# A seven-product w_up: another order of the products, w_down groups between the units, x1 kept in DRAM

## The chip, the cores and the metric

The kernel runs on one core of one Trainium2 chip. Its engines are TensorE (PE in the profile; PEld is its weight load), VectorE (DVE), ScalarE (ACT), GpSimd (POOL) and SyncE (SP, which issues most loads). The metric is the device time of one execution in microseconds.

## The reference

One layer of a hybrid backbone is computed for 128 context tokens and 512 latent tokens, 640 rows of 1024 channels: adaLN-modulated norm, retention and grouped-query attention side by side, a merge, an output projection w_out with a gated residual; then a second modulated norm and a gated MLP with a width-3 convolution between up- and down-projection; a final norm. The change lies in the second half:

```python
xs = xs + g1 * y                                        # y = merged mixers @ w_out
h = rmsnorm(xs, norm2_g[l]) * (1.0 + sc2) + sh2         # h2 in the kernel
xs = xs + g2 * conv_ffn(h, w_up[l], conv_w[l], conv_b[l], w_down[l])
y_sample = rmsnorm(xs, final_g)

def conv_ffn(h, w_up, conv_w, conv_b, w_down):          # D_FF = 2816
    u = h @ w_up                                        # 1024 x 5632: halves a and g
    up = jnp.pad(u, ((0, 0), (1, 1), (0, 0)))
    uc = conv_w[0] * up[:, :L] + conv_w[1] * up[:, 1:L + 1] + conv_w[2] * up[:, 2:L + 2] + conv_b
    a, g = jnp.split(uc, 2, axis=-1)
    return (jax.nn.silu(g) * a) @ w_down
```

## The kernel before, in words

Every float32 product is made of three matmuls on a high and a low part of each operand (high x high, high x low, low x high). A weight block arrives by SyncE as a `raw` tile of 1 MB (two of them). The high part is a ScalarE cast (L146); the low part `raw - hi` is either a VectorE subtraction (L151) or, in the mode "dma", a scaled ScalarE copy (L148) and an accumulating DMA from GpSimd's queue (L149). High and low parts lie in `wh` tiles of [128, 1024], of which there are eight.

*w_out, second half, and h2.* For each of five token tiles (t = 0 is the context) a PSUM bank collects eight k steps, four from each half of the weights (`out_half(t, h)`). `evac_out` multiplies by the gate and adds to x1, the residual; `h2_norm` scales the row; `h2_trans` transposes it on TensorE (L1047), and ScalarE and VectorE write the modulated high and low parts (L1055 to L1059) into `h2`, from which w_up reads. Meanwhile the w_up blocks of the first pair of feature tiles (`whl`, `w_g`) are loaded and split, and the pair's products (`up_cols`, L1118 to L1120) are mixed with the last transposes.

*w_up.* The 22 feature tiles of each half (i = 0 for a, i = 1 for g) are worked in eleven pairs p. Pairs 0 and 1 are plain products. VectorE forms sums of blocks of h2 (`diff`, `neg_sum`, L1168 to L1174) and for p = 2 to 10 a pair and half is one *unit*: a product of 2x2 blocks done with seven products of half size instead of eight. Each product is 12 matmuls of 322 columns (L1307, L1309, L1310) on a weight operand that VectorE and ScalarE prepare (L1285, L1288, L1293; for products 2 and 3 ScalarE and GpSimd's DMA, L1290, L1291). Products 1, 6, 7 and 4 are added up in one bank without clearing it, and between any two ScalarE has to copy what stands there (L1312, L1316, L1320, L1324), so that each next product waits for a copy. Product 2 has a bank of its own, 5 and 3 share one. The order is 1, 5, 6, 2, 7, 3, 4.

*conv and gate.* When both i of a feature tile are there, `conv` (one ScalarE pass, two on VectorE) and `gate` follow: tanh, two VectorE multiplications (L1139, L1140), the high part by ScalarE (L1141) and the low part by GpSimd (L1142).

*w_down.* Four feature tiles (two for p = 0 and 1 alone) are a group of rows; for each of two column halves five banks of 128 x 512 are summed over them, and `down_add` multiplies each bank by the gate and adds it to x1. All groups but the last stand in a list with the w_up groups: `plain(1,0)`, the two halves of the first w_down group, `plain(1,1)`, then unit(p,0), for odd p both halves of a w_down group, unit(p,1). A final w_down group and the closing norm (L1236 and following) come after the list.

*Order.* TensorE runs this list as written (`manual_schedule`). After each item `pump` loads the next block and prepares weights ahead as long as eight `wh` slots allow, and one waiting conv or gate is taken from the queue `later`. The order on the other engines is a scheduler's.

## Time and profile before

| | us |
|---|---|
| median of 3 runs | 1221.78 (1220.73 to 1225.39) |
| profiled execution | 1221.7, its span on the core 1219.9 |
| mean granted TensorE clock | 0.990 |
| busy: PE, DVE, ACT, POOL | 1165.2, 773.4, 553.9, 201.5 |
| w_out second half, h2, first pair of w_up | 709 to 772.5 |
| gate rows on TensorE | 772.5 to 776 |
| plain(1,0) | 776 to 794.6 |
| first w_down group | 794.6 to 808.6 |
| plain(1,1) | 808.6 to 822.9 |
| 18 units and four w_down groups of ten banks | 822.9 to 1176.5 |
| last w_down | 1176.5 to 1204.6 |
| closing norm and outputs | 1204.6 to 1219.9 |

Times within the span count from its start. A tile has its pool's name, its own and a number (mm7.mm.40 is the 40th bank of the pool mm7). Engines with a q (POOLq) are their queues of DMAs.

### The profile page before, as it was taken

How to read it: one execution, taken by the hardware profiler on the slowest of the kernel's cores; microseconds unless marked ns; L12 is line 12 of the kernel's file. 1: busy time of each engine (PE TensorE's matmuls, PEld its weight loads, DVE VectorE, ACT ScalarE, POOL GpSimd, SP SyncE). 2: the span in 40 equal slices, each digit the busy share in tenths (PEclk: the TensorE clock that was granted, in tenths of full speed). 3: DMA queues.
4: the chain of work that ended last, by engine and by line, in shares of the span. 5: the costliest groups of instructions: out<-in, count | busy, mean ns of one | idle time of the engine just before them, and what ended most of it. 6: DMA issues, size and time to landing. Idle time of an engine off the chain costs nothing.

```text
span 1219.9 us, 18328 instructions
## 1 busy us (share of the span) xinstructions
PE 1165.2 (96%) x7329; PEld 1046.6 (86%) x7329; DVE 773.4 (63%) x1450; ACT 553.9 (45%) x999; POOL 201.5 (17%) x184
## 2 busy tenths in 40 slices
PE   4999999999999999999999997999999999999994
PEld 3788899999988888789999887999898898898984
DVE  5676977763344346544233368889788787797877
ACT  4355655551223234434222334637457266474553
POOL 0032200000022000231111110203223122122222
PEclk9999999999999999999999998999999999999998
DMA  8822111126544422022222417235756568457522
GB/s 285 277 96 70 36 35 35 36 74 213 183 164 139 154 80 75 4 70 68 71 70 70 155 39 86 78 87 113 173 104 137 115 118 182 97 110 175 105 70 86
DMA packets 127413, 132.20 MB, mean 108 GB/s; under 512 B 25936, under 2 KB 96672, under 8 KB 127328
## 3 DMA queue, kind: packets, MB, share of 16 engines
q1 hardware_dynamic: 104432, 109.01, 28.3%
q0 software_dynamic: 22176, 20.71, 11.6%
q8 instruction: 57, 0.93, 0.3%
q10 hardware_dynamic: 720, 1.31, 0.3%
q14 instruction: 28, 0.23, 0.1%
HBM read 107.69 MB, written 3.41 MB: 91 GB/s over the span
## 4 chain that ended last, share of the span: by engine, by line
PE 74%; DVE 13%; ACT 4%; issue 4%; DMA 3%; POOL 1%; SPq 0%; DVEq 0%; ACTq 0%; POOLq 0%
DVE x1.u1.1_6381 L1218 1%; DMA weights.raw.199_7284<-in_w_up 1%; DMA weights.wh.244_8024<-weights.raw.232_7804 1%; DMA weights.raw.366_10197<-in_w_down 0%; DMA weights.raw.324_9445<-in_w_down 0%; DMA weights.raw.282_8693<-in_w_down 0%; DMA xin.u1.1_112<-in_x_sample 0%; DMA weights.raw.404_10963<-in_w_down 0%; POOL f0.s.5_3525 L901 0%; DVE weights.raw.216_7428 L1285 0%; DVE gt.gt0.5_7252 L1170 0%; DVE gt.gt0.5_7252 L1168 0%; DVE x1.u1.1_6381 L1236 0%; ACT const.u1.1_70 L1320 0%; PE mm1.mm.11_318 L158 0%
## 5 line engine op out<-in xcount | busy, mean ns | idle before, releaser
L790 POOL TENSOR_TENSOR ret.r2k.6_3635<-ret.u5.5_3528,ret.u1.1_3521 128x256 f32<-128x256 f32 x2 | 1.4, 740 | 205.1 <-ACT ret.u5.5_3528 L786 205.1
L1321 DVE TENSOR_TENSOR t7.u3.3_6921<-t7.u3.3_6921,const.u1.1_70 128x322 f32<-128x322 f32 x9 | 8.1, 895 | 10.0 <-ACT const.u1.1_70 L1320 10.0
L524 POOL TENSOR_TENSOR p1.u1.1_618<-p1.u3.3_622,p1q.u1.1_612 128x512 f32<-128x512 f32 x1 | 1.3, 1337 | 59.3 <-DMA p1.vc.6_627<-in_cache_v 59.3
L839 DVE SCALAR_TENSOR_TENSOR ret2.u1.1_4322<-ret2.u1.1_4322,const.u14.14_94 64x128 f32<-64x128 f32 x24 | 6.8, 338 | 6.6 <-ACT ret2.u1.1_4322 L832 6.5
L151 DVE TENSOR_TENSOR weights.wh.183_6567<-weights.raw.181_6564,weights.wh.182_6566 128x1024 fp32r<-128x1024 f32 x1 | 1.2, 1224 | 14.3 <-ACT weights.wh.182_6566 L146 14.3
L1233 POOL TENSOR_TENSOR x1.u1.1_6381<-x1.u1.1_6381,weights.raw.409_10973 128x512 f32<-128x512 f32 x5 | 7.5, 1493 | 15.2 <-ACT x1.tm.122_11171 L1223 7.1
L355 PE MATMUL mm1.mm.1_180<-const.u1.1_70,xin.u1.1_112 128*128 128x128 f32 x4 | 1.1, 435 | 9.1 <-DVE xin.u1.1_112 L348 9.1
L841 DVE SCALAR_TENSOR_TENSOR ret2.u1.1_4322<-ret2.u1.1_4322,const.u14.14_94 64x128 f32<-64x128 f32 x24 | 6.6, 382 | 4.8 <-ACT ret2.u1.1_4322 L834 4.8
L792 DVE TENSOR_TENSOR ret.u5.5_3528<-ret.u5.5_3528,ret.u1.1_3521 128x512 f32<-128x512 f32 x5 | 3.5, 693 | 9.4 <-POOL ret.r2k.8_3706 L790 3.3
L792 DVE TENSOR_TENSOR ret.u4.4_3527<-ret.u4.4_3527,ret.u1.1_3521 128x512 f32<-128x512 f32 x5 | 3.5, 692 | 9.0 <-POOL ret.r2k.11_3886 L790 4.7
L392 ACT CAST acts.u1.1_100<-f0.s.1_113 128x640 fp32r<-128x640 f32 x4 | 2.9, 728 | 12.8 <-DVE f0.s.1_113 L390 12.8
L355 PEld LDWEIGHTS mm1.mm.1_180<-const.u1.1_70,xin.u1.1_112 128*128 128x128 f32 x4 | 0.7, 217 | 9.3 <-DVE xin.u1.1_112 L348 9.3
L149 POOL DMA_DIRECT2D weights.wh.207_7299<-weights.raw.200_7286 x1 | 0.8, 849 | 45.1 <-ACT weights.wh.207_7299 L148 45.1
L828 POOL DMA_DIRECT2D out_new_state_ret_fwd<-ret.r2k.25_4345 x1 | 0.7, 654 | 43.8 <-ACT ret.r2k.25_4345 L827 43.8
L151 DVE TENSOR_TENSOR weights.wh.108_4352<-weights.raw.106_4349,weights.wh.107_4351 128x1024 fp32r<-128x1024 f32 x1 | 1.2, 1225 | 10.3 <-ACT weights.wh.107_4351 L146 10.3
L901 POOL TENSOR_TENSOR f0.s.5_3525<-f0.s.5_3525,ret2.ny20.11_4904 128x512 f32<-128x512 f32 x5 | 6.0, 1236 | 9.1 <-DVE ret2.ny20.11_4904 L218 9.1
L392 ACT CAST acts.u1.1_100<-f0.s.2_114 128x640 fp32r<-128x640 f32 x4 | 2.9, 730 | 9.8 <-DVE f0.s.2_114 L390 9.8
L258 DVE COPY mod2.wr.9_4312<-aux3.aux.15_4279 128x128 f32<-128x128 f32 x1 | 0.3, 291 | 10.9 <-PE aux3.aux.15_4279 L255 10.9
L493 ACT ACTIVATE f0.s.3_724<-f0.s.3_724,p1q.ny20.11_892 128x128 f32<-128x128 f32 x20 | 6.0, 388 | 2.5 <-DVE p1q.ny20.11_892 L216 2.5
L146 ACT CAST weights.wh.112_4507<-weights.raw.111_4505 128x1024 fp32r<-128x1024 f32 x1 | 1.1, 1050 | 13.3 <-PE mm3.mm.36_4220 L159 13.3
L924 POOL TENSOR_TENSOR f0.s.5_3525<-f0.s.5_3525,ret.r2k.56_4795 128x512 f32<-128x512 f32 x1 | 1.3, 1284 | 33.5 <-DVE ret.r2k.56_4795 L922 33.5
L974 DVE SCALAR_TENSOR_TENSOR rt.thr.6_5935<-rt.thr.6_5935,mm3.mm.71_6118 128x320 f32<-128x320 f32 x1 | 0.5, 489 | 9.6 <-PE mm3.mm.71_6118 L195 9.6
(7045 smaller groups left out, 4947.9 us busy)
## 6 DMA issues: line engine op xcount, KB each, us to landing
xin.u1.1_112<-in_x_sample SPq DMA_DIRECT2D x4, 512.0 KB
p0.u5.5_130<-in_w_mod SPq DMA_DIRECT2D x2, 1024.0 KB
p0.u6.6_135<-in_w_mod SPq DMA_DIRECT2D x2, 1024.0 KB
p0.u7.7_138<-in_w_mod SPq DMA_DIRECT2D x2, 1024.0 KB
mod.wm.2_2921<-in_w_mod SPq DMA_DIRECT2D x1, 2048.0 KB
mod.wm.4_3072<-in_w_mod SPq DMA_DIRECT2D x1, 2048.0 KB
mod.wm.6_3227<-in_w_mod SPq DMA_DIRECT2D x1, 2048.0 KB
mod.wm.8_3382<-in_w_mod SPq DMA_DIRECT2D x1, 2048.0 KB
```

The source lines that it names most:

```text
L151: (lo_eng or V).tensor_sub(lo, rv, hi.bitcast(F32))
L355: nc.tensor.transpose(ps[:, j * P:(j + 1) * P], xin[:, t, k * P:(k + 1) * P], ident)
L392: nc.scalar.copy(hT[0][:, k, :], xk)
L493: nc.scalar.activation(x[:, j], x[:, j], AF.Copy, scale=rstd[:, j:j + 1])
L790: nc.gpsimd.tensor_mul(sw[:, :, b * 32:(b + 1) * 32], xs, r1[:, t, 1:2, b * 32:(b + 1) * 32].to_broadcast([P, 8, 32]))
L792: V.tensor_mul(z, z, r1[:, t, 0:1, :].to_broadcast([P, 8, 64]))
L839: V.scalar_tensor_tensor(Ss[0:64, hh, st + 1, j], Ss[0:64, hh, st, j], cdsel[0:64, h:h + 1], Ss[0:64, hh, st + 1, j], op0=ALU.mult, op1=AL ...
L841: V.scalar_tensor_tensor(Ss[64:128, hh, 2 - st, j], Ss[64:128, hh, 3 - st, j], cdsel[64:128, h:h + 1], Ss[64:128, hh, 2 - st, j], op0=ALU. ...
L901: nc.gpsimd.tensor_mul(ov, ov, rso[:, 4 * t:4 * t + 4].unsqueeze(2).to_broadcast([P, 4, P]))
L1218: V.tensor_add(x1[:, t, gs], x1[:, t, gs], tm)
L1233: nc.gpsimd.tensor_mul(x1[:, t, lo], x1[:, t, lo], fg[:, lo])
L1321: V.tensor_sub(u[1][:, hi_u], u[1][:, hi_u], u3[i])
```

## The change

1. w_out's second half goes in plain order: after the first two half banks each tile's two halves follow one another. The part `whl` of the first w_up block is split into 1280 and 768 columns and made during the first two tiles, the latter in a new kind of x1 tile (`x_row`, four of 768 columns, which also hold the conv results); it takes no `wh` slots any more.
2. As soon as a tile of x1 is final after w_out it is also written to DRAM (`x1d`, from GpSimd's queue). The first w_down group overwrites x1 by a ScalarE copy (`step` 0), the next groups add to it (`step` 1), and the group at p = 9 adds, multiplies once by the gate and adds the part of `x1d` that GpSimd's queue reads back (`step` 2). The last group after the list keeps `down_add`. x_tmp has three buffers instead of four.
3. The low part of a gate is made on VectorE instead of GpSimd. The gates of odd pairs run after the second w_down half.
4. The low parts of the plain(1,0) and plain(1,1) weights are made in the mode "dma".
5. The two halves of a w_down group stand apart: plain(1,0), half, plain(1,1), half; unit(p,0), half, unit(p,1), half. Preparations are sorted by the first use.
6. The products go 1, 5, 6, 2, 3, 7, and product 4 is held until two items of the following group have run.

In the changed file lines move by up to 25: L1030 is L1036, L1036 is L1042, L1058 and L1059 are L1064 and L1065; of a unit's copies L1312, L1314, L1316, L1320 and L1324 are L1329, L1331, L1333, L1337 and L1342, its casts and DMAs L1288 to L1291 are L1305 to L1308; the conv's ScalarE pass L1128 is L1133.

VectorE where token tile 3 is normed (nm1, ni1, ny1, nt1 belong to its rsqrt; tm.43 is an x_tmp tile of token tile 4), before:

```order
L1036 TENSOR_TENSOR x1.u2.2_6382<-x1.u2.2_6382 128x1
L1030 TENSOR_TENSOR x1.tm.43_6859<-mm3.mm.88_6773,gate.u1.1_5311 128x512
L206 TENSOR_SCALAR x1.nm1.39_6832<-x1.u2.2_6382 128x1
L151 TENSOR_TENSOR weights.wh.202_7289<-weights.raw.199_7284,weights.wh.201_7288 128x1024
L207 TENSOR_SCALAR x1.ni1.40_6833<-x1.nm1.39_6832 128x1
L1031 TENSOR_TENSOR x1.u1.1_6381<-x1.u1.1_6381,x1.tm.43_6859 128x512
L208 TENSOR_SCALAR x1.ny1.41_6834<-x1.ni1.40_6833 128x1
L209 TENSOR_SCALAR x1.nm1.39_6832<-x1.nm1.39_6832 128x1
```

and after the change:

```order
L1042 TENSOR_TENSOR x1.u2.2_6382<-x1.u2.2_6382 128x1
L1064 CAST acts.u1.1_100<-x1.row.40_6818 128x4x128
L206 TENSOR_SCALAR x1.nm1.41_6826<-x1.u2.2_6382 128x1
L1065 TENSOR_TENSOR acts.u2.2_101<-x1.row.40_6818,acts.u1.1_100 128x4x128
L207 TENSOR_SCALAR x1.ni1.42_6827<-x1.nm1.41_6826 128x1
L208 TENSOR_SCALAR x1.ny1.43_6828<-x1.ni1.42_6827 128x1
L209 TENSOR_SCALAR x1.nm1.41_6826<-x1.nm1.41_6826 128x1
L212 SCALAR_TENSOR_TENSOR x1.nt1.44_6829<-x1.ny1.43_6828,x1.nm1.41_6826 128x1
```

The subtraction L151 on the weights of plain(1,0) no longer stands inside this norm.

ScalarE at the start of unit(6,1) (mm.40 is its shared bank, mm.41 that of product 5, mm.37 the shared bank of unit(6,0)), before:

```order
L1312 COPY t7.u2.2_6920<-mm7.mm.40_9335 128x322
L1314 ACTIVATE t7.u4.4_6922<-mm7.mm.41_9353 128x322
L1316 ACTIVATE t7.u4.4_6922<-mm7.mm.40_9335 128x322
L1288 CAST weights.wh.318_9350<-weights.raw.308_9161 128x512
L1288 CAST weights.wh.319_9368<-weights.raw.308_9161 128x512
```

and after the change:

```order
L1329 COPY t7.u2.2_6928<-mm7.mm.40_9263 128x322
L1305 CAST weights.wh.314_9278<-weights.raw.308_9162 128x512
L1331 ACTIVATE t7.u4.4_6930<-mm7.mm.41_9281 128x322
L1305 CAST weights.wh.315_9296<-weights.raw.298_8969 128x512
L1342 COPY t7.u1.1_6927<-mm7.mm.37_9144 128x322
L1305 CAST weights.wh.317_9316<-weights.raw.308_9162 128x512
L1133 ACTIVATE x1.row.82_9319<-t7.u1.1_6927,t7.u5.5_6935 128x641
L1333 ACTIVATE t7.u4.4_6930<-mm7.mm.40_9263 128x322
```

The copies after products 1 and 6 of a unit (L1329, L1333) now have product 5's and the previous unit's product 4's between them.

GpSimd around the w_down group of p = 7 (raw.316 and raw.324, in the changed kernel raw.316 and raw.327, are the two halves of the w_down weights), before:

```order
L149 DMA weights.wh.326_9523<-weights.raw.316_9308 128x1024
L1142 TENSOR_TENSOR gt.gt1.20_9440<-t7.cv.42_9310,gt.gt0.19_9439 128x641
L149 DMA weights.wh.328_9528<-weights.raw.316_9308 128x1024
L1142 TENSOR_TENSOR gt.gt1.20_9440<-t7.cv.43_9331,gt.gt0.19_9439 128x641
L149 DMA weights.wh.331_9596<-weights.raw.324_9445 128x1024
L149 DMA weights.wh.333_9601<-weights.raw.324_9445 128x1024
L1291 DMA weights.wh.338_9702<-weights.raw.329_9532 128x4x128
```

and after the change:

```order
L149 DMA weights.wh.322_9438<-weights.raw.316_9299 128x1024
L149 DMA weights.wh.324_9443<-weights.raw.316_9299 128x1024
L1308 DMA weights.wh.331_9586<-weights.raw.325_9447 128x4x128
L1308 DMA weights.wh.332_9636<-weights.raw.325_9447 128x4x128
L149 DMA weights.wh.335_9673<-weights.raw.327_9470 128x1024
L149 DMA weights.wh.337_9678<-weights.raw.327_9470 128x1024
```

The gates' low parts have left the queue, and the two halves' DMAs have those of the unit between them. The core of the diff:

```diff
+    dp = Pool("spill", space=bass.MemoryType.DRAM)
+    x1d = dp([P, NT, DM])
...
     def x_tmp():
-        return x1p([P, 512], tag="tm", bufs=4)
+        return x1p([P, 512], tag="tm", bufs=3)
+
+    def x_row(dtype=F32):
+        return x1p([P, 768], dtype, tag="row", bufs=4)
...
-    whl = [[x[:, :1024] for x in gt_flat(F32R)]]
-    nc.scalar.copy(whl[0][0], raw[:, :1024])
-    V.tensor_sub(whl[0][1], raw[:, :1024], whl[0][0].bitcast(F32))
+    whl = [[x[:, :1280] for x in gt_flat(F32R)], [x_row(F32R) for _ in range(2)]]
...
         for t in range(NT):
-            if t in (1, 2, 3):
-                out_half(t + 1, 0)
+            if t >= 2:
+                out_half(t, 0)
             out_half(t, 1)
             evac_out(1)(t, bank[t])
-            if t == 3:
-                whl.append([wp([P, 1024], F32R, tag="wh", bufs=8) for _ in range(2)])
-                nc.scalar.copy(whl[1][0], raw[:, 1024:])
-                V.tensor_sub(whl[1][1], raw[:, 1024:], whl[1][0].bitcast(F32))
+            nc.gpsimd.dma_start(x1d[:, t, :], x1[:, t, :])
+            if t in (0, 1):
+                rv = raw[:, 1280 * t:1280 + 768 * t]
+                nc.scalar.copy(whl[t][0], rv)
+                V.tensor_sub(whl[t][1], rv, whl[t][0].bitcast(F32))
...
-        nc.gpsimd.tensor_sub(r[1], ca, r[0].bitcast(F32))
+        V.tensor_sub(r[1], ca, r[0].bitcast(F32))
...
+    def down_sum(ps, t, c0, step):
+        gs = slice(c0, c0 + 512)
+        if step == 0:
+            nc.scalar.copy(x1[:, t, gs], ps)
+            return
+        V.tensor_add(x1[:, t, gs], x1[:, t, gs], ps)
+        if step == 2:
+            xr = x_tmp()
+            nc.gpsimd.dma_start(xr, x1d[:, t, gs])
+            V.tensor_mul(x1[:, t, gs], x1[:, t, gs], gb[:, t == 0, gs])
+            V.tensor_add(x1[:, t, gs], x1[:, t, gs], xr)
...
-            st["w"] = w_split(st["raw"], 8, 256)
+            st["w"] = w_split(st["raw"], 8, 256, "dma")
...
-        order = (1, 5, 6, 2, 7, 3, 4)
+        order = (1, 5, 6, 2, 3, 7, 4)
...
-    groups = [plain_group(1, 0)] + down_groups([0, 1]) + [plain_group(1, 1)]
+    d0 = down_groups([0, 1], 0)
+    groups = [plain_group(1, 0), d0[0], plain_group(1, 1), d0[1]]
     for p in range(2, NF // 2):
-        groups.append(unit_group(p, 0))
+        groups += [unit_group(p, 0), unit_group(p, 1)]
         if p % 2:
-            groups += down_groups(list(range(2 * p - 4, 2 * p)))
-        groups.append(unit_group(p, 1))
-    seq = [x for g in groups for x in g[2]]
+            d = down_groups(list(range(2 * p - 4, 2 * p)), 2 if p == 9 else 1, (2 * p + 1, 2 * p))
+            groups = groups[:-1] + [d[0], groups[-1], d[1]]
+    seq, held = [], []
+    for _, _, items in groups:
+        for x in items[:-1] if len(items) == 7 else items:
+            seq.append(x)
+            held = [(n - 1, y) for n, y in held]
+            if held and held[0][0] == 0:
+                seq.append(held.pop(0)[1])
+        if len(items) == 7:
+            held.append((2, items[-1]))
+    seq += [y for _, y in held]
...
+    preps.sort(key=lambda z: z[4])
```

More of the change, by code (lines that the diff above doesn't have):

```diff
@@ L1134, in gate @@
     def gate(f):
+        if f // 2 not in gts:
+            gts[f // 2] = gt_pair()
         r = [x[:, f % 2, :641] for x in gts[f // 2]]
@@ L1322, in go @@
                     V.memset(u[1][:, 642:643], 0)
+                    later.append(lambda: conv(f0_ + 1, i))
                 elif m == 4:
@@ L1326, in go @@
                     later.append(lambda: conv(f0_, i))
-                    if i:
-                        later.append(lambda: gate(f0_))
+                    if i and (p % 2 == 0):
+                        later.extend([lambda: gate(f0_ + 1), lambda: gate(f0_)])
                 else:
@@ L1358, in go @@
                     down_mm(ps, t, fs, st["w"])
-                    down_add(ps, t, g * 512)
+                    down_sum(ps, t, g * 512, step)
+                    if g and t == NT - 1:
+                        later.extend([lambda f=f: gate(f) for f in after])
                 return go
@@ L1384, in pump @@
             elif preps and preps[0][0] < loaded and sum(z for z, last in live if last >= n) + preps[0][2] <= 8:
-                gi, fn, tiles, last = preps.pop(0)
+                gi, fn, tiles, last, _ = preps.pop(0)
                 fn()
```

17 lines of the change are left out of this document (5 added, 12 removed).

## The prediction

> **What bounds the kernel now.** I read the page, then windows by stage, then what TensorE waits for.
>
> ```profile
> PE 1165.2 (96%) x7329; PEld 1046.6 (86%) x7329; DVE 773.4 (63%) x1450; ACT 553.9 (45%) x999; POOL 201.5 (17%) x184
> PE 74%; DVE 13%; ACT 4%; issue 4%; DMA 3%; POOL 1%; SPq 0%; DVEq 0%; ACTq 0%; POOLq 0%
> ```
>
> In the windows a row has the stretch, its length, the busy time of PE, PEld, DVE, ACT and POOL, the granted clock (PEclk, third from the end), the DMA share and GB/s:
>
> ```profile
> 740.00:760.00 20.00, 16.72 (x114) 16.72 (x115) 16.87 (x49) 6.25 (x17) 0.00 (x0) 0.83 0.73 48
> 776.00:794.60 18.60, 16.18 (x99) 15.92 (x98) 12.16 (x13) 10.55 (x15) 7.90 (x4) 0.91 0.56 141
> 822.90:1176.50 353.60, 341.85 (x1993) 314.17 (x1993) 285.64 (x449) 205.22 (x353) 88.98 (x69) 1.00 0.61 129
> 1176.50:1204.60 28.10, 28.10 (x134) 23.08 (x132) 22.48 (x41) 11.24 (x23) 9.61 (x6) 1.00 0.00 1
> ```
>
> PE is the bound, 96% busy, and both kernels give it the same number of instructions. Only its waits, and the granted clock behind them, can be won. The order of the engines' instructions is the same up to about 700 us. From there PE is short of its time in the h2 stage (740 to 760), in the first plain w_up product (776 to 794.6) and in the unit stage; the last w_down has no wait, and neither that nor the closing norm changes.
>
> ```profile
> PE aux3.aux.97_6973 L1047 <- DVE gt.gt1.2_6393 L1038: 4.8, 1, 4.8
> PE mm7.mm.5_7312 L1120 <- DVE weights.wh.204_7293 L151: 2.4, 1, 2.4
> PE aux3.aux.95_6864 L1047 <- DVE gt.gt0.1_6392 L1038: 1.4, 1, 1.4
> ...
> PE mm7.mm.55_10223 L1307 <- ACT const.u1.1_70 L1320: 1.1, 1, 1.1
> ...
> PE mm7.mm.40_9335 L1307 <- ACT t7.u2.2_6920 L1312: 1.1, 1, 1.1
> ```
>
> The first three waits belong to the two early stages. The other two kinds are the units': product 6 waits until ScalarE has copied product 1 out of the bank (L1312), product 4 until it has copied product 7 (L1320). What this costs is read from lengths:
>
> ```profile
> 863.30:891.50 28.20, 28.12 (x122) 22.50 (x121) 20.44 (x31) 7.21 (x12) 2.36 (x3) 1.00 0.55 123
> 945.30:973.20 27.90, 27.90 (x123) 22.60 (x122) 20.68 (x33) 7.38 (x12) 2.34 (x3) 1.00 0.54 125
> 973.20:985.60 12.40, 12.40 (x86) 12.40 (x85) 9.54 (x17) 8.16 (x16) 3.84 (x3) 1.00 0.64 128
> 985.60:998.80 13.20, 12.68 (x85) 12.42 (x85) 13.16 (x21) 9.79 (x18) 3.97 (x3) 1.00 0.47 107
> 998.80:1013.00 14.20, 12.90 (x86) 12.38 (x85) 12.20 (x23) 9.19 (x18) 4.08 (x4) 1.00 0.53 109
> 1013.00:1027.20 14.20, 13.13 (x87) 12.56 (x86) 9.99 (x14) 12.19 (x18) 6.20 (x6) 1.00 0.95 183
> 1027.20:1055.00 27.80, 27.80 (x121) 22.53 (x121) 20.67 (x33) 7.33 (x12) 2.30 (x3) 1.00 0.53 123
> 1109.10:1136.90 27.80, 27.80 (x121) 22.52 (x121) 20.66 (x33) 7.33 (x12) 2.31 (x3) 1.00 0.53 123
> ```
>
> The four w_down stretches take 28.2 + 27.9 + 27.8 + 27.8 = 111.7 us, the 18 units the rest of 353.6: 241.9. A unit right behind w_down takes 12.40 without a wait (seven products of 1.77, below), the others 13.2 to 14.2. Excess: 241.9 - 18 x 12.40 = 18.7 us. Listed waits alone show less, because each matmul row reaches over the start of the next.
>
> **The change, part by part.** *w_out and h2.* The weights of the first plain product (weights.raw.199) land at 737.14, VectorE's low-half subtraction L151 waits for the cast of them, and the norm of token tile 3 is queued behind it on VectorE:
>
> ```profile
> 729.84 7.30 DMA weights.raw.199_7284<-in_w_up
> 738.30 1.23 DVE L151 TENSOR_TENSOR weights.wh.202_7289<-weights.raw.199_7284,weights.wh.201_7288 128x1024 fp32r<-128x1024 f32 x1 [1.47 <-ACT weights.wh.201_7288 L146]
> 743.30:747.40 4.10, 4.10 (x20) 4.10 (x21) 4.03 (x17) 1.50 (x4) 0.00 (x0) 0.50 0.83 6
> 720.30:752.00 31.70, 25.49 (x154) 22.78 (x153) 26.53 (x85) 14.38 (x30) 2.00 (x6) 0.89 0.65 70
> 751.99 0.45 PE aux3.aux.99_7049 L1047 x4
> ```
>
> Behind the 4.8 us of waiting the clock is 0.50 for 4.1 us, which loses 2.05. In the new order that L151 is gone (the low half is a ScalarE pass and a GpSimd DMA that nothing on VectorE waits for), and tiles 2 and 3 end half a w_out bank earlier. ScalarE, 14.38 busy of 31.70, has room for the pass. Recoverable: 1.4 + 4.8 + 2.05 = 8.2 us. But VectorE is the next limit: of 31.70 us up to the last tile's transposes (751.99) it is busy 26.53, and 1.23 of that leaves: 720.3 + 25.3 = 745.6. PE's own work there is 25.49, 2.05 of it lost to the clock, so it would be ready at 743.7 and is not the limit; w_g's low halves (one landed 9.3 us after its issue, row below) may come a microsecond late, which these 1.9 us cover. Gain 751.99 - 745.6 = **6.4** (bounds: 3, if half moves to the next tile's norm, and 8.2). I take VectorE's value, as it leaves that engine no idle time.
>
> *First plain product.* The 2.4 us wait for L151 (which sits behind VectorE's operand sums) and the half clock behind it:
>
> ```profile
> 779.58 1.15 DVE weights.wh.204_7293 L151
> 781.70:785.10 3.40, 3.40 (x15) 3.40 (x14) 3.40 (x4) 1.24 (x3) 3.40 (x2) 0.50 0.92 240
> weights.wh.196_6936<-weights.raw.194_6933 POOLq DMA_DIRECT2D x1, 512.0 KB, 9.3
> ```
>
> 2.4 + 1.7 = **4.1**. The raw slot is free early now, all four low halves can be made during the h2 stage, and even a DMA of 9.3 us has 30. Bounds 0 and 4.1; I take the upper one, since nothing that it waits for is near.
>
> *Units.* Order 1 5 4' 6 2 3 7 (4' of the unit before) puts two products, 3.5 us, between any two of the shared bank instead of one. Behind a w_down group only product 5 stands between 1 and 6, as in the 12.40 unit of before, which shows no wait; 7 and 4 are then two w_down banks apart.
>
> ```profile
> 985.59 0.31 PE L1307 MATMUL mm7.mm.37_9190<-acts.u1.1_100,weights.wh.301_9048 128*128 128x322 f32 x1
> 987.37 0.30 PE L1307 MATMUL mm7.mm.38_9212<-sums.u1.1_6910,weights.wh.302_9066 128*128 128x322 f32 x1
> L148 ACT ACTIVATE weights.wh.326_9523<-weights.raw.316_9308 128x1024 fp32r<-128x1024 f32 x1 | 1.1, 1067 | 0.0
> L1312 ACT COPY t7.u2.2_6920<-mm7.mm.34_9051 128x322 f32<-128x322 f32 x1 | 0.4, 427 | 0.7 <-PE mm7.mm.34_9051 L1310 0.7
> ```
>
> A product takes 1.77 (985.59 to 987.37, less the odd 0.01). The copy takes 0.43 and may stand behind one or two weight passes of up to 1.07 on ScalarE: 2.6 at most, under 3.5. Only two links keep a stall: the last unit's 4 directly behind its 7 (0.8: copy, semaphore and restart), and four times the gate of the pair before a w_down group, whose low half I find 0.3 late (1.2). I leave 1.7 for what I cannot place: 18.7 - 0.8 - 1.2 - 1.7 = **15.0** (bounds 0 and 18.7).
>
> *VectorE's load.* In the unit stage w_down's 80 two-input operations become 60 (three groups with one add, p = 9 with three, ScalarE copies in the plain stage): -20 x 0.68. Sixteen gate low halves of 641 columns come to it from GpSimd, as long as a gate multiplication: +16 x 0.82. But GpSimd's were not free for it:
>
> ```profile
> 989.47 0.68 DVE L1285 TENSOR_TENSOR weights.raw.300_9046<-weights.raw.300_9046 128x512 f32<-128x512 f32 x1
> 990.08 0.82 DVE L1140 TENSOR_TENSOR t7.cv.36_8825<-t7.cv.36_8825,t7.cv.38_9163 128x641 f32<-128x641 f32 x1
> 992.25 2.66 DVE L1285 TENSOR_TENSOR weights.raw.300_9046<-weights.raw.300_9046 128x512 f32<-128x512 f32 x2
> 991.80 1.97 POOL L1142 TENSOR_TENSOR gt.gt1.18_9156<-t7.cv.36_8825,gt.gt0.17_9155 128x641 fp32r<-128x641 f32 x1 [6.54 <-ACT gt.gt0.17_9155 L1141]
> ```
>
> Two adds that take 0.68 alone took 2.66 beside it, 1.3 more than both. The two moves cancel (-13.6 and +13.1), and up to 16 x 1.3 of blocking leaves: VectorE's 285.64 us fall by some 15 (an estimate), to 270 of 338 us, and the unit that had it busy 13.16 of 13.20 is relieved. Bounds: a loss of 0.82 in each unit that runs at the limit, four of them, 3.3, and a gain that the units' term already holds. I take 0. The x1 spill is five GpSimd DMAs of 512 KB, read by nobody for 300 us. Of its ten reads of 256 KB three are issued at once; each other waits for the add three banks earlier (3 x 2.78 = 8.3 us) and should land in under the 7.8 of a 512 KB one below. On GpSimd's queue the low halves of the next units stand behind these reads, which wait for VectorE's adds of w_down's banks; those come 14 us before the halves are needed. Cost 0; without that cover seven reads could hold p = 9's banks 2 to 3 us each, 14 to 21 us.
>
> *w_down starts.* Four double groups become eight single ones, each needing its two low halves from GpSimd DMAs:
>
> ```profile
> 1021.67 0.85 POOL L149 DMA_DIRECT2D weights.wh.328_9528<-weights.raw.316_9308  x1
> ...
> weights.wh.249_8097<-weights.raw.240_7941 POOLq DMA_DIRECT2D x1, 512.0 KB, 8.8
> weights.wh.326_9523<-weights.raw.316_9308 POOLq DMA_DIRECT2D x1, 512.0 KB, 7.8
> weights.wh.331_9596<-weights.raw.324_9445 POOLq DMA_DIRECT2D x1, 512.0 KB, 5.2
> ```
>
> Before, the second half of the group at 1027.20 was issued 5.5 us ahead of it (1021.67), is needed some 1.6 us into it (half a bank), and its stretch shows no wait. Now its slot is freed by the third product of the unit ahead (5.3), ScalarE's copy and two passes follow (about 2.1), so it is issued at 7.4 of that unit and lands, with 5.2, at 12.6; needed at 12.4 + 1.6 = 14.0. Before the second group the unit ahead has six products (10.6), the slot is freed at 3.5, issue is at about 5.3, landing at 10.5, needed at 12.2. With 8.8 they would be 2.2 and 1.9 late. The two long landings are of DMAs beside which a 1 MB raw load was moving; in the new order these loads start earlier. I take 0 (bounds 0 and 4 x 2.2 + 4 x 1.9 = 16.4, without a clock loss).
>
> Sum: 6.4 + 4.1 + 15.0 = 25.5; 1221.7 (the profiled execution, 0.08 under the median) - 25.5 = **1196**.
>
> **Rivals.** *VectorE binds the units.* The 13.16 of 13.20 speaks for it, the 2.66 row against. If all units stay at 13.2, they gain 241.9 - 18 x 13.2 = 4.3: 1221.7 - 14.8 = 1207. *Low halves land moderately late*, 1.5 us at each of eight starts, 12: 1208. *The early stages give half* (another norm waits): 1201. *Slower:* the low halves land 9 us or more after their issue, so each of eight starts is 2.4 late, and, as behind the 2.4 us wait above, half clock adds 1.7: 8 x 4.1 = 32.8, 1229. The 9.3 and 8.8 rows speak for it, the 5.2 row and four starts without a wait against. It decides from a landing of 9.0 (5.2 + 1.4 of margin + 2.4). That the change fails to space the products is no rival of weight: the order of the instructions shows them spaced.
>
> The Trainium skill (TensorE: Matmul & The Clock Gate, Part 1: The HAM clock gate) has the clock fall to half after an idle window of about 3.4 us. By that the 2.4 us stalls would cost themselves alone, 19 us, and this rival would end at 1215. The trace differs: 0.50 stood behind a gap of 2.42 us, so the row's price stays.
>
> **How the numbers follow.** Forecast 0.60 (own range 1191 to 1202), VectorE 0.12, moderately late 0.12, early stages 0.09, slower 0.07. The range 1190 to 1211 holds all but the last and the edges. About 0.5% (6.1 us) is what a measurement tells from no change: faster 0.87, same 0.06 (the upper edges of the second and third), slower 0.07.
>
> **What would show it.** Right: unit windows of 12.4 throughout, no wait of PE on the bank's copies, the transposes of the last tile near 745.6, PEclk 1.00 at the first plain product. Wrong: waits of PE on L149's DMAs or on the gate's low half at w_down's first bank, VectorE busy over 12 us in a unit, or waits on x_tmp's reads in p = 9.

## The result and the profile after

The changed kernel takes 1201.69 us, median of 4 runs (1199.89 to 1202.9), against 1221.26 of the kernel before on the same chip (1219.59 to 1225.39): ratio 0.9834, 95% interval 0.9805 to 0.9862. The profiled execution took 1202.29 with a span of 1200.5 us. The page, busy times and the chain that ended last:

```profile
PE 1160.6 (97%) x7329; PEld 1043.8 (87%) x7329; DVE 736.5 (61%) x1428; ACT 567.1 (47%) x1013; POOL 173.9 (14%) x181
PE 82%; DVE 8%; ACT 3%; issue 2%; DMA 2%; POOL 1%; SPq 0%; DVEq 0%; ACTq 0%; POOLq 0%
```

TensorE's share of the chain rose from 74% to 82%, and VectorE's busy time fell by 37 us. What TensorE still waits for from 700 us on (total, times, longest):

```profile
PE mm7.mm.64_10766 L1324 <- ACT const.u1.1_70 L1337: 2.1, 1, 2.1
PE aux3.aux.99_7057 L1053 <- DVE gt.gt0.1_6395 L1044: 0.9, 1, 0.9
PE acc7.acc.46_10513 L159 <- DMA weights.wh.379_10430<-weights.raw.369_10202: 0.8, 1, 0.8
PE mm7.mm.61_10648 L1324 <- ACT const.u1.1_70 L1337: 0.6, 1, 0.6
PE mm7.mm.5_7315 L1123 <- ACT gate.u1.1_5311 L275: 0.2, 1, 0.2
```

The 4.8 and the 2.4 us waits of the early stages and nearly all waits on the shared bank's copies are gone. Four are left that matter; all but the second stand at the end of the unit stage, after 1110 us. The windows of the early stages (the columns are those of the prediction) and of all 18 units with the w_down groups between them:

```profile
720.30:744.70 24.40, 23.54 (x155) 21.06 (x154) 23.76 (x77) 16.35 (x33) 7.62 (x14) 1.00 0.92 166
769.40:786.00 16.60, 16.56 (x106) 16.17 (x107) 11.29 (x13) 10.57 (x16) 1.67 (x2) 1.00 0.31 73
812.10:1157.60 345.50, 341.12 (x1996) 314.84 (x1995) 259.55 (x444) 208.35 (x349) 60.90 (x57) 1.00 0.63 137
```

Up to the last transposes VectorE is busy 23.76 of 24.40 us: it is the limit there, with TensorE close behind it (23.54), and the clock stays at 1.00. The first plain product runs without a stall at full clock. In the units VectorE has 259.55 us of work instead of 285.64.

Where the time went, by starts of matmuls in the two traces:

| | before | after | gain |
|---|---|---|---|
| last tile's transposes (aux.99) | 751.83 | 744.68 | 7.1 |
| plain(1,0) starts | 776.04 | 769.44 | 6.6 |
| units start | 822.89 | 812.14 | 10.75 |
| units to the end of the last w_down | 381.74 | 373.15 | 8.6 |
| end of the last w_down to the end | 15.3 | 15.2 | 0.1 |

10.75 + 8.6 + 0.1 = 19.4, the difference of the profiled executions (1221.7 - 1202.29). Counted from the start of w_out's second half (690.13 and 690.64), the units start after 132.8 us before and 121.5 after, which is 11.3; half a microsecond was lost earlier, where the kernels do not differ. In what follows the *excess* of a product or bank is the time from its start to the next one's, less 1.765 us for a product or 2.79 for a bank of twelve matmuls, the values that undisturbed ones have in all traces. Before, it added up to 19.6 us in the units and 0.1 in the w_down groups between them.

*The last unit's product 4.* ScalarE's queue there, and the DMA in it from the chain of waits:

```profile
1147.09 1.06 ACT L146 CAST weights.wh.400_10911<-weights.raw.397_10905 128x1024 fp32r<-128x1024 f32 x1
1152.95 1.04 ACT L146 CAST weights.wh.403_10917<-weights.raw.402_10915 128x1024 fp32r<-128x1024 f32 x1 [4.80 <-DMA weights.raw.402_10915<-in_w_down]
1153.90 0.42 ACT L1337 COPY const.u1.1_70<-mm7.mm.64_10766 128x322 f32<-128x322 f32 x1
1147.70 5.16 DMA weights.raw.402_10915<-in_w_down
1154.40:1157.60 3.20, 3.20 (x12) 3.20 (x13) 2.22 (x5) 1.79 (x2) 0.00 (x0) 0.52 0.00 0
```

The copy after product 7 (L1337) could have run at 1151.4, when product 7 had ended. But the scheduler put the cast of the last w_down weights ahead of it. ScalarE ran the two in that order, and the cast waited 4.80 us for its load. TensorE waited 2.1 us and then ran twelve matmuls at clock 0.52: 2.1 + 1.5 + 0.4 in the banks behind = 4.0 us.

The load itself was late. It was issued at 1147.70, into the buffer of raw.382, when the last low half made from raw.382 had landed (5.4 us after its issue). That one stood behind ScalarE's passes, and these behind a gate's cast that waited 2.16 us for VectorE:

```profile
1138.63 0.73 ACT L1148 CAST gt.gt0.25_10640<-x1.row.96_10330 128x641 fp32r<-128x641 f32 x1 [2.16 <-DVE x1.row.96_10330 L1147]
1142.27 1.55 POOL L1308 DMA_DIRECT2D weights.wh.394_10721<-weights.raw.382_10453  x1
```

VectorE is full there: from the third bank of p = 9's second w_down half (1118.67) to the end of product 7 it is busy 32.0 of 32.7 us.

*The first bank of each w_down group* (the matmuls of acc.11, and VectorE's low part of the gate that they need):

```profile
849.15 0.83 DVE L1149 TENSOR_TENSOR gt.gt1.12_8009<-x1.row.66_7855,gt.gt0.11_8008 128x641 fp32r<-128x641 f32 x1 [0.25 <-ACT gt.gt0.11_8008 L1148]
850.03 0.50 PE L160 MATMUL acc7.acc.11_8080<-weights.wh.239_7978,gt.gt1.12_8009 128*128 128x512 f32 x1
```

The bank starts at 847.55 and reaches the last feature tile before its gate is done. This costs 0.71 to 0.74 us in each of the four groups, 2.9.

### The profile page after: what moved, and what is told of

The parts are those of the page before. It is cut to its first block, busy times and chain, and to the rows that moved or that the text cites. A ratio compares the mean times of both kernels' runs of the same rounds, so it can differ in the third digit from the quotient of the medians.

```text
span 1200.5 us, 18330 instructions
## 1 busy us (share of the span) xinstructions
PE 1160.6 (97%) x7329; PEld 1043.8 (87%) x7329; DVE 736.5 (61%) x1428; ACT 567.1 (47%) x1013; POOL 173.9 (14%) x181
## 4 chain that ended last, share of the span: by engine, by line
PE 82%; DVE 8%; ACT 3%; issue 2%; DMA 2%; POOL 1%; SPq 0%; DVEq 0%; ACTq 0%; POOLq 0%
DMA weights.wh.379_10430<-weights.raw.369_10202 1%; DVE acts.u2.2_101 L1065 1%; DVE x1.u1.1_6381 L1224 1%; DMA xin.u1.1_112<-in_x_sample 0%; DMA weights.wh.394_10721<-weights.raw.382_10453 0%; DMA weights.raw.402_10915<-in_w_down 0%; POOL f0.s.5_3525 L901 0%; DVE acts.u1.1_100 L1064 0%; DVE x1.u1.1_6381 L1037 0%; DVE x1.u1.1_6381 L1254 0%; DVE gt.gt0.5_7260 L1175 0%; PE mm1.mm.11_318 L158 0%; PE mm7.mm.46_9644 L1327 0%; PE mm7.mm.34_8912 L1327 0%; PE mm7.mm.22_8180 L1327 0%
## 5 line engine op out<-in xcount | busy, mean ns | idle before, releaser
L1338 DVE TENSOR_TENSOR t7.u4.4_6930<-t7.u4.4_6930,const.u1.1_70 128x322 f32<-128x322 f32 x9 | 4.5, 496 | 10.1 <-ACT const.u1.1_70 L1337 10.1
L151 DVE TENSOR_TENSOR weights.wh.183_6570<-weights.raw.181_6567,weights.wh.182_6569 128x1024 fp32r<-128x1024 f32 x1 | 1.2, 1226 | 14.3 <-ACT weights.wh.182_6569 L146 14.3
L151 DVE TENSOR_TENSOR weights.wh.108_4352<-weights.raw.106_4349,weights.wh.107_4351 128x1024 fp32r<-128x1024 f32 x1 | 1.2, 1226 | 10.3 <-ACT weights.wh.107_4351 L146 10.3
L1235 DVE TENSOR_TENSOR x1.u1.1_6381<-x1.u1.1_6381,gate.u1.1_5311 128x512 f32<-128x512 f32 x10 | 6.7, 687 | 0.0
L1338 DVE TENSOR_TENSOR t7.u3.3_6929<-t7.u3.3_6929,const.u1.1_70 128x322 f32<-128x322 f32 x9 | 4.4, 494 | 3.4 <-ACT const.u1.1_70 L1337 3.4
```

The costliest lines, as they stand in the source:

```text
L151: (lo_eng or V).tensor_sub(lo, rv, hi.bitcast(F32))
L1235: V.tensor_mul(x1[:, t, gs], x1[:, t, gs], gb[:, t == 0, gs])
L1338: V.tensor_sub(u[1][:, hi_u], u[1][:, hi_u], u3[i])
```

## The experiments

Times are compared with the kernel before on the same chip (1220.75 to 1221.0). The last column, from the start of the units to the end of the last w_down, is read from one trace of each version. The start of the units lies between 809.2 and 813.8 in the versions of the changed kernel, moved by the first 700 us, which no run edits: from the start of w_out's second half to the units they all take 121.4 to 121.5 us, but for the run that edits this part. The column has a chance in it too, of some 2 us: whether half clock follows the wait at the last unit's product 4. In the run with the plain low halves on VectorE, which edits nothing in this stretch, that wait was 1.9 us, the clock behind it stayed at 1.00, and the stretch is 2.0 us shorter than in the changed kernel. Up to p = 9's second w_down group, the stretch is the same within 0.1 us wherever it is not edited (298.0 to 298.1).

| run | us | ratio, 95% interval | units to end of last w_down |
|---|---|---|---|
| changed kernel again | 1201.44 | 0.9834 (0.9818 to 0.9851) | 373.1 |
| last unit in the old order, first form | 1199.57 | 0.9819 (0.9805 to 0.9834) | 370.1 |
| last unit in the old order | 1198.35 | 0.9814 (0.9800 to 0.9829) | 369.9 |
| two feature tiles swapped | 1197.49 | 0.9807 (0.9786 to 0.9828) | 370.2 |
| x1 added by the DMA | 1199.27 | 0.9822 (0.9807 to 0.9836) | 370.5 |
| old product order everywhere | 1223.99 | 1.0021 (1.0004 to 1.0038) | 393.5 |
| gate's low part on GpSimd | 1206.18 | 0.9873 (0.9858 to 0.9888) | 378.0 |
| plain low halves on VectorE | 1204.43 | 0.9866 (0.9850 to 0.9883) | 371.1 |
| before with the new product order alone | 1234.35 | 1.0122 (1.0103 to 1.0141) | 395.0 |
| old order and gate on GpSimd | 1232.74 | 1.0102 (1.0079 to 1.0124) | 403.0 |
| three edits together | 1197.63 | 0.9816 (0.9796 to 0.9836) | 369.4 |
| last unit, swap, reads by SyncE | 1197.01 | 0.9809 (0.9793 to 0.9824) | 368.6 |

**The changed kernel again**, without an edit.

> The changed kernel again, as the measure for the other runs on this chip: about 1201 us, with the same four places of loss: 4.0 us at the last unit's held product 4, about 0.7 us in the first bank of each of the four first w_down halves, 1.1 us in the first bank of the second half at p = 9, 1.2 us inside the last unit.

The same result, and the same places: excess 8.5 us in the units and groups, again 2.0 us ahead of the last product 4.

**The last unit in the old order, product 4 not held.** First form:

```diff
-        order = (1, 5, 6, 2, 3, 7, 4)
+        order = (1, 5, 6, 2, 7, 3, 4) if p == NF // 2 - 1 and i else (1, 5, 6, 2, 3, 7, 4)
...
-        for x in items[:-1] if len(items) == 7 else items:
+        hold = len(items) == 7 and gn < len(groups) - 1
+        for x in items[:-1] if hold else items:
```

> The last unit keeps the old order 1 5 6 2 7 3 4 and its 4 is not held, so that product 3 stands between 7 and 4, and the copy after 7 no longer stands behind a weight cast that waits for the last w_down load. Theory (the 2.1 us wait of the last product 4 and the half clock behind it are a queue place on ScalarE): 3 to 4 us faster than the changed kernel, no wait on L1337 there, clock 1.00. Rival (the end is bound by that last load and by the closing norm anyway): within 1 us, the wait turns into one on the last w_down's second weights.

In this form the convolution of the last feature tile is queued before product 3 has been added, so that part of its input is left out. The second form queues it after product 3:

```diff
+        old = p == NF // 2 - 1 and i == 1
...
-                    later.append(lambda: conv(f0_ + 1, i))
+                    if not old:
+                        later.append(lambda: conv(f0_ + 1, i))
...
                 else:
                     V.tensor_sub(u[1][:, lo_u], u[1][:, lo_u], ps)
+                    if old:
+                        later.append(lambda: conv(f0_ + 1, i))
```

> As e1_last4, with the conv of the second feature tile put behind product 3, where that order makes its input ready. From the start of the units to the end of the last w_down the changed kernel takes 373.1 us. Theory (queue place on ScalarE): 3 to 3.5 less, no wait on L1337 at the last product 4, 0.6 us at the last w_down's second weights. Rival: within 1 us.

Both shorten the stretch by 3.1 to 3.2 us. The wait on L1337 and the half clock are gone; what the last w_down waits for instead is small:

```profile
PE acc7.acc.46_10513 L159 <- DMA weights.wh.379_10430<-weights.raw.369_10202: 0.6, 1, 0.6
PE acc7.acc.52_10936 L159 <- DVE t7.u4.4_6930 L1351: 0.5, 1, 0.5
PE mm7.mm.65_10780 L1325 <- DVE t7.u1.1_6927 L1336: 0.3, 1, 0.3
```

So nearly all of the 4 us was this one copy behind a cast that waited for its load.

**The first bank of a w_down group takes its last two feature tiles in the other order** (only the first half's first bank of the four groups):

```diff
-        for n, f in enumerate(fs):
+        seq_ = list(enumerate(fs))
+        if swap:
+            seq_ = seq_[:2] + seq_[:1:-1]
+        for z, (n, f) in enumerate(seq_):
...
-                    down_mm(ps, t, fs, st["w"])
+                    down_mm(ps, t, fs, st["w"], swap=len(fs) == 4 and g == 0 and t == 0)
```

> In the first bank of each first w_down half the last two feature tiles change places, so that the one whose gate is made last is used last. Theory (that gate's high and low half are late there): 4 x 0.7 = 2.9 us faster than the changed kernel, first bank 2.8 instead of 3.5 us. Rival (the bank is slow because its weights' low half lands late): no change, 3.5 us again.

The four first banks take 2.97 us again instead of 3.66 to 3.69, which shows that the late gate was the cause: weights that land late would have left the bank as it was. The stretch is 2.9 shorter too, but that it equals the expected 2.9 is chance, since two waits moved with the edit:

```profile
PE acc7.acc.46_10513 L159 <- DMA weights.wh.379_10430<-weights.raw.369_10202: 2.3, 1, 2.3
PE mm7.mm.64_10766 L1327 <- ACT const.u1.1_70 L1340: 1.6, 1, 1.6
1153.40:1155.30 1.90, 1.89 (x12) 1.89 (x13) 1.37 (x4) 1.47 (x2) 0.00 (x0) 1.00 0.00 0
```

TensorE arrives earlier at p = 9's second group and waits 2.3 us for the low half instead of 0.8, with half clock behind it: this group lost 3.1 us. The last product 4 still waits 1.6, but this time the clock behind it is 1.00, and the stretch behind p = 9's group is 3.3 shorter (54.9 us instead of 58.2).

**x1's part added by an accumulating DMA** instead of a read and an addition on VectorE:

```diff
-            xr = x_tmp()
-            nc.gpsimd.dma_start(xr, x1d[:, t, gs])
             V.tensor_mul(x1[:, t, gs], x1[:, t, gs], gb[:, t == 0, gs])
-            V.tensor_add(x1[:, t, gs], x1[:, t, gs], xr)
+            nc.gpsimd.dma_start(x1[:, t, gs], x1d[:, t, gs], accum_op=ALU.add)
```

> At p = 9 the x1 part comes from DRAM by an accumulating DMA straight into x1, instead of a read into x_tmp and a VectorE addition: ten VectorE operations of 0.68 less there, and no read that waits for a buffer. Theory (three operations a bank fill VectorE from 1116 to 1142 and the prefetched reads stand ahead of the weights' low halves): 1.5 to 2.5 us faster than the changed kernel, no wait for the low half at the second w_down half of p = 9. Rival (the low half is late because of the 1 MB loads beside it, and the accumulating DMAs move as many bytes): within 1 us.

The stretch is 2.6 shorter. The wait at mm.61 is gone and the one ahead of the last product 4 fell to 1.3, without half clock. Ten additions less on VectorE let the last low half from raw.382 start at 1140.65 instead of 1142.27 and the load of the last weights at 1146.79 instead of 1147.70, which is the 0.8 us of the wait; another 1.5 is the half clock that did not follow. The low half of p = 9 is later, not earlier, so the reads' wait for a free buffer is not what delays it:

```profile
PE mm7.mm.64_10746 L1322 <- ACT const.u1.1_70 L1335: 1.3, 1, 1.3
PE acc7.acc.46_10503 L159 <- DMA weights.wh.379_10420<-weights.raw.369_10202: 1.2, 1, 1.2
```

**The changed kernel with the old product order, none held:**

```diff
+        old = True
...
-        order = (1, 5, 6, 2, 3, 7, 4)
+        order = (1, 5, 6, 2, 7, 3, 4) if old else (1, 5, 6, 2, 3, 7, 4)
...
-        for x in items[:-1] if len(items) == 7 else items:
+        for x in items:
             seq.append(x)
...
-        if len(items) == 7:
-            held.append((2, items[-1]))
```

(The convolution of the second tile is again queued behind product 3.)

> The changed kernel with the products in the old order 1 5 6 2 7 3 4 and none held; all else stays. Theory (the spacing by two products is what took the units' waits away): of 18 units, ten are not right behind a w_down half; at the old excess of 1.3 us each they take 13 us more, less the 4 us of the last product 4: 9 us slower than the changed kernel, with waits on the copies after 1 and 7 again. Rival (the waits went because VectorE and ScalarE have less to do, by the additions and the gate's low half): less than 3 us slower, or faster by the 4 us.

It is 22 us slower than the changed kernel (ten runs, 1219.2 to 1229.3), which neither account foresaw. The waits, and ScalarE at the second of them:

```profile
PE mm7.mm.58_10402 L1325 <- ACT const.u1.1_70 L1338: 7.3, 1, 7.3
PE mm7.mm.22_8186 L1325 <- ACT const.u1.1_70 L1338: 5.1, 1, 5.1
PE mm7.mm.34_8918 L1325 <- ACT const.u1.1_70 L1338: 3.4, 1, 3.4
PE mm7.mm.46_9650 L1325 <- ACT const.u1.1_70 L1338: 2.7, 1, 2.7
...
875.89 0.62 ACT L1306 CAST weights.wh.257_8253<-weights.raw.251_8184 128x512 fp32r<-128x512 f32 x1 [7.99 <-DMA weights.raw.251_8184<-in_w_up]
876.41 0.42 ACT L1338 COPY const.u1.1_70<-mm7.mm.22_8186 128x322 f32<-128x322 f32 x1
876.90:880.20 3.30, 3.30 (x12) 3.30 (x13) 3.27 (x8) 0.62 (x1) 0.00 (x0) 0.50 0.47 140
```

All four stand in the unit ahead of a second w_down half. It is the picture of the last unit: a cast on ScalarE that waits 7.99 us for a load (10.25, 6.34 and 5.57 at the other three), and behind it the copy that product 4 needs; then half clock. Of the fourteen other units thirteen have no excess at all and the last has 0.7, although in them too the old order leaves one product between two uses of the bank. In the changed kernel, then, the waits of before would have gone in these units without the new order.

**The gate's low part on GpSimd again:**

```diff
-        V.tensor_sub(r[1], ca, r[0].bitcast(F32))
+        nc.gpsimd.tensor_sub(r[1], ca, r[0].bitcast(F32))
```

> The changed kernel with the gate's low half on GpSimd again. Theory (the spacing covers VectorE's blocked operations; only the first banks of the w_down halves feel it): the low half takes 1.6 instead of 0.8 us, so 4 x 0.8 = 3 us slower, VectorE additions beside it at 1.3 us again. Rival (GpSimd's hold on VectorE was the units' cost): 8 us slower or more, waits inside the units. Third: the same time or faster, since VectorE at p = 9 is relieved.

The stretch is 4.9 us longer, between the two accounts. At the first bank of every w_down group TensorE now waits 0.9 us for GpSimd (five rows like the first one here), and waits on VectorE and on a copy appear in units:

```profile
PE acc7.acc.11_8080 L160 <- POOL gt.gt1.12_8009 L1149: 0.9, 1, 0.9
PE mm7.mm.65_10780 L1324 <- DVE t7.u1.1_6927 L1335: 1.4, 1, 1.4
PE mm7.mm.26_8438 L1324 <- ACT t7.u3.3_6929 L1331: 1.0, 1, 1.0
```

**The plain weights' low halves on VectorE again:**

```diff
-            st["w"] = w_split(st["raw"], 8, 256, "dma")
+            st["w"] = w_split(st["raw"], 8, 256)
```

> The changed kernel with the low halves of the two plain products' weights on VectorE again (L151). Theory (that work inside the norms, and its wait, made the h2 and first plain stages long): the last tile's transposes 2 to 6 us later than 744.7, units start 3 to 8 us later than 811.7 to 812.1. Rival (w_out's plain order and the early raw slot made the gain): units start within 1.5 us.

```profile
PE aux3.aux.99_7057 L1053 <- DVE gt.gt0.1_6395 L1044: 2.9, 1, 2.9
```

The wait ahead of the last transposes is 2.9 instead of 0.9, and the units start at 813.78 instead of 812.14. Counted from the start of w_out's second half the units start after 123.5 us instead of 121.5. So L151 accounts for 2.0 of the early gain. The first plain product does not wait for L151 here either, so the 2.4 us of before there were won by the earlier weights: their load is issued at 708.96 instead of 729.84, and the second L151 runs at 743.22 instead of 779.50. The order of w_out's tiles and these earlier weights give the rest of the gain, and no run parts them. The median lies further off, 3.0 us above the changed kernel's (1204.43 to 1201.44): the profiled execution was the fastest of the four (1201.85), with a mean granted clock of 0.994 against 0.991 in the others.

**The kernel before with the new product order alone:**

```diff
-        order = (1, 5, 6, 2, 7, 3, 4)
+        order = (1, 5, 6, 2, 3, 7, 4)
...
-    seq = [x for g in groups for x in g[2]]
+    seq, held = [], []
+    for _, _, items in groups:
+        for x in items[:-1] if len(items) == 7 else items:
+            seq.append(x)
+            held = [(n - 1, y) for n, y in held]
+            if held and held[0][0] == 0:
+                seq.append(held.pop(0)[1])
+        if len(items) == 7:
+            held.append((2, items[-1]))
+    seq += [y for _, y in held]
```

(The convolution and gate of the second tile are queued behind product 3, which now comes ahead of 7.)

> The kernel before, with only the new product order 1 5 6 2 3 7 and product 4 held until two items of the next group have run; weights, low halves, w_down groups and x1 stay as they were. It separates the two accounts of why the waits on the shared bank's copies went. Spacing (the prediction): two products, 3.5 us, stand between any two of the bank, a copy comes 2.6 us late at most, so the 18.7 us of excess in the units nearly goes: 12 to 18 us faster than before, 1204 to 1209, and the 1.1 us waits of the units are gone. Queues (the rival, after the run that kept the change but took the old order and had no wait in 14 of 18 units): the waits came from VectorE and ScalarE being held up by GpSimd's work and by the double w_down groups; spacing alone does little: under 6 us faster, over 1215, with waits still standing in units.

The time is wrong for both accounts: 13 us slower. The place is clear. The units' excess fell from 19.6 to 2.7, so spacing alone does remove the copy waits, and it removes more than the 12 us that were asked of it. But the w_down groups have 29.5 us of excess instead of 0.1, nearly all in their first two banks. The waits at the group of p = 7, and ScalarE there:

```profile
PE acc7.acc.31_9581 L158 <- ACT gt.gt0.19_9420 L1141: 3.6, 1, 3.6
PE acc7.acc.31_9581 L159 <- DMA weights.wh.326_9517<-weights.raw.316_9308: 1.0, 1, 1.0
PE acc7.acc.31_9581 L160 <- POOL gt.gt1.20_9421 L1142: 0.6, 1, 0.6
...
1030.49 1.04 ACT L146 CAST weights.wh.330_9627<-weights.raw.324_9445 128x1024 fp32r<-128x1024 f32 x1 [2.52 <-DMA weights.raw.324_9445<-in_w_down]
1032.71 0.73 ACT L1141 CAST gt.gt0.19_9420<-t7.cv.43_9367 128x641 fp32r<-128x641 f32 x1
```

Holding product 4 makes the gate of its tile late, and the gate's high part (L1141) then stands behind a cast of the *second* half's weights, which waits for its load. In the four groups together TensorE waits 8.9 us for that high part and 6.9 us for low halves of weights, which GpSimd issues later relative to the group than before (wh.326 5.3 us ahead of it instead of 9.4); at p = 3 there is only the latter. In the changed kernel that half comes a whole unit later, and its casts do not stand there. The new order gains nothing without the separated groups.

**Old product order and GpSimd's low part together** (the edits of the two runs above):

> The changed kernel with the old product order, nothing held, and the gate's low half on GpSimd again. The old order by itself cost 20 us at the four places ahead of a w_down half and left 14 units without excess. If GpSimd's hold on VectorE (0.68 us adds that took 2.66 for two) was what made the copies late before, waits of about 1 us on the copies after products 1 and 7 come back in most of those units: some 12 us or more of new excess there, about 1236 or more. If the separation of the w_down groups and the smaller number of additions was the reason, those units stay at 12.4 and only the gate's later low halves are paid, 5 us as in the run with that part alone: about 1229.

Between the two: 1232.74 (two runs), the stretch 9.5 us longer than with the old order alone. Waits on the copy after product 6 are back in the first units of even pairs (1.8, 1.3 and 1.3 us, and 0.8 in the very first unit), not in most units; and at p = 7 a product 4 waits 2.6 us for the copy after product 7, behind a cast that waits 2.72 us for its load. The first of the waits after product 6 on three engines and in the waits:

```profile
899.26 1.76 POOL L1149 TENSOR_TENSOR gt.gt1.14_8407<-x1.row.69_8076,gt.gt0.13_8406 128x641 fp32r<-128x641 f32 x1
900.81 1.73 POOL L1149 TENSOR_TENSOR gt.gt1.14_8407<-x1.row.70_8098,gt.gt0.13_8406 128x641 fp32r<-128x641 f32 x1
899.33 4.49 DVE L1303 TENSOR_TENSOR weights.raw.256_8237<-weights.raw.256_8237 128x512 f32<-128x512 f32 x2
903.13 0.62 ACT L1306 CAST weights.wh.266_8429<-weights.raw.256_8237 128x512 fp32r<-128x512 f32 x1 [3.06 <-DVE weights.raw.256_8237 L1303]
PE mm7.mm.25_8414 L1325 <- ACT t7.u3.3_6929 L1334: 1.8, 1, 1.8
```

Two additions of 0.69 us take 4.49 beside GpSimd's two subtractions (the first alone 3.76, until 0.55 after the second subtraction has ended), ScalarE's cast waits 3.06 for them, and the bank's copies queue behind it. That GpSimd holds VectorE up, and that this makes copies late, is shown; how the rest of before's 19.6 us divides between the double groups and the additions now gone is not.

**Three edits together** (last unit, swap, accumulating DMA):

> The changed kernel with three edits together: the last unit in the old order with nothing held, the last two feature tiles of the first bank of each w_down group swapped, and the x1 part added by an accumulating DMA. Alone they shortened the stretch from the first unit to the end of the last w_down (373.1) to 369.9, 370.2 and 370.5. If the three losses are separate (the late copy in the last unit, the gate's late halves, VectorE's load at the end) the gains add up but for the last wait that two of them share: 366 to 367.5, 1194.5 to 1196. If what is won at the first banks is lost again at the late low half of p = 9 (its wait grew to 2.3 with the swap alone): 369 or more, 1197.5 or more.

369.4: the gains did not add up, though not for the reason given. The wait at p = 9 is 1.0, the first banks are clean, but in this version the scheduler again put a cast of the last weights ahead of the copy after the last product 7, and TensorE waited 1.8:

```profile
1145.77 1.04 ACT L146 CAST weights.wh.403_10897<-weights.raw.402_10895 128x1024 fp32r<-128x1024 f32 x1 [4.22 <-DMA weights.raw.402_10895<-in_w_down]
1146.72 0.42 ACT L1339 COPY const.u1.1_70<-mm7.mm.64_10746 128x322 f32<-128x322 f32 x1
```

**Last unit, swap, and x1's reads issued by SyncE:**

```diff
-            nc.gpsimd.dma_start(xr, x1d[:, t, gs])
+            nc.sync.dma_start(xr, x1d[:, t, gs])
```

> The changed kernel with the last unit in the old order and the swapped tiles, and the ten reads of the x1 part issued by SyncE instead of GpSimd. It tells what makes the low half of p = 9's second w_down group late (TensorE's wait 0.8 in the changed kernel, 2.3 with the swap, 1.2 with an accumulating DMA). If its place on GpSimd's queue behind the reads does it, that wait goes (under 0.3) and the time is 1194 to 1196. If the bytes that move at the same moment do it (x1 reads and the 1 MB weight loads), the wait stays at 0.8 or more, and loads of SyncE behind the reads may come later: 1197 to 1200.

Time and wait are those of the second account. TensorE waits 2.2 us for p = 9's low half, as with the swap alone (2.3), though no read is left on GpSimd's queue. GpSimd's issues of the second low half at p = 7 and p = 9, their time to landing, and the windows of each pair's first w_down half (banks 1 to 5):

```profile
1024.73 0.86 POOL L149 DMA_DIRECT2D weights.wh.337_9678<-weights.raw.327_9470  x1 [2.14 <-ACT weights.wh.337_9678 L148]
1105.10 0.86 POOL L149 DMA_DIRECT2D weights.wh.379_10430<-weights.raw.369_10202  x1 [1.01 <-DVE t7.u2.2_6928 L1339]
weights.wh.337_9678<-weights.raw.327_9470 POOLq DMA_DIRECT2D x1, 512.0 KB, 5.1
weights.wh.379_10430<-weights.raw.369_10202 POOLq DMA_DIRECT2D x1, 512.0 KB, 6.8
1003.40:1017.30 13.90, 13.90 (x66) 11.44 (x65) 12.12 (x22) 6.27 (x10) 1.29 (x1) 1.00 0.41 142
1081.50:1095.40 13.90, 13.90 (x65) 11.46 (x64) 13.30 (x25) 6.15 (x10) 1.29 (x1) 1.00 0.58 181
```

At p = 7 the issue is 5.2 us ahead of its group (1029.94), at p = 9 2.8 us ahead (1107.94), and it lands 1.7 us later besides. The place on GpSimd's queue is ruled out. VectorE, with three operations for each bank, is nearly full at p = 9 (13.30 of 13.90), and weight preparation falls behind it; that this alone makes the issue late is argued, not shown. In the changed kernel itself the issue is 5.2 us ahead (1105.01 for 1110.21) and the landing takes 7.8 us while three reads move, so there the bytes are the likelier cause. This point stays open.

No version beats the others clearly: 1197.0 to 1198.4 us for the last-unit edit, the swap and their combinations, some 3 to 4.5 us under the changed kernel, with overlapping intervals.

## Why the prediction was right, and where it was not

The forecast of 1196 was 5.7 us too low; the range 1190 to 1211 held 1201.69, and the forecast's own range (1191 to 1202) held it only just. The time alone would have spoken for the rival "the early stages give half" (1201); the trace rules it out, since these stages gave all that was forecast and the units gave less.

*h2 stage and first plain product: right.* 6.4 + 4.1 = 10.5 forecast, 10.75 measured. The last transposes start at 744.68 (745.6 forecast); 0.5 of their 7.1 us is lost again before plain(1,0). VectorE was taken as the next limit, and the window shows it busy 23.76 of 24.40, where the forecast had 25.3. The 1.7 us of half clock in the 4.1 need not have been there to win: the kernel before with the new product order has the same wait there (2.4), and the clock behind it stays at 1.00. Of the edits there, the mode of the plain weights' low halves is worth 2.0.

*Units: right in mechanism, 15.0 forecast and 8.6 measured.* The waits on the copies went, and the order alone is enough for that (19.6 to 2.7 in the kernel before). It was not the only way: in the changed kernel 13 units stay clean in the old order too, which the prediction did not see. What is left, in its own terms (19.6 - 8.6 = 11.0, against 3.7 of its 18.7):

| | forecast | measured |
|---|---|---|
| last unit's product 4 | 0.8 | 4.0 |
| gate's low part, four groups | 1.2 | 2.9 |
| p = 9's late low half (w_down starts) | 0 | 1.1 |
| the product 4 held into the last unit, late copy | 0 | 0.9 |
| unplaced | 1.7 | 2.1 |

The step that failed is the bound on a copy: 0.43 behind one or two passes of 1.07, "2.6 at most". It counted how long the passes ahead run, not that one of them may itself wait for a load: 4.80 us in the changed kernel, 7.99 in the old order. In this execution the clock then nearly doubled the damage. The gate's 0.3 was a sum of durations on a VectorE that was taken as free between them.

*VectorE's load: right in sign.* 285.64 fell to 259.55, 26 us where 15 was estimated. Up to p = 9 VectorE did not come to bind the units: in the fullest stretch of twenty products between two w_down groups it is busy 28.8 of 35.4 us, 10 in a unit's time. Behind p = 9's second w_down half it did, with 23.56 of 24.26 us in the last thirteen products, 12.7 in a unit's time: the sign "over 12 us in a unit" came there. The cost taken as 0 was a part of the 4.0 and, it seems, of the 0.9 above.

*w_down starts: 0 forecast.* Right for seven of eight; the low halves land in 4.5 to 6.1 us there. The rivals of late low halves (1208 and 1229) did not come. At p = 9, where the reads of x1 fall, 6.9 and 7.8 us and one wait of 0.8: the sign "waits at p = 9" was named, with the wrong victim, the weights' low half instead of the banks' adds.

*The clock.* The prediction priced half clock behind a 2.4 us wait by its row. The row's price holds: clock 0.52 behind 2.1 us here, 0.50 behind 5.1 us with the old order; it stayed 1.00 behind 1.6 us. But the price is not due each time: it stayed 1.00 behind 2.45 and 2.87 us too (below).

## What to carry to other kernels

Bound a late operation on an in-order engine by what the operations ahead of it *wait for*, not only by how long they run: a weight cast whose load is still moving, placed by a scheduler ahead of a small PSUM copy, cost more with the old order in the changed kernel (some 27 us of excess at four places, the half clock included) than the waits that the new order was to remove (19.6). Two remedies for one wait do not add up, and one may need the other: the new order alone lost 13 us, the rest of the change without it about 3 (ratio 1.0021, with the early stages' gain of 11 in it), both together won 20. When a stage is judged by its excess over undisturbed instructions, group by group, an end-to-end time that looks like "no effect" shows its two halves, and a gain that looks like the expected one (the swap's 2.9) can turn out to be three others.
